# Turning keys and queries in 32 by 32 blocks on VectorE, with the stores to DRAM putting the blocks in place

## The chip, the cores and the metric

The kernel runs on one core of one Trainium2 chip. The metric is the device time of one execution in microseconds. The kernel before took 2872.75 us, the median of three runs from 2871.84 to 2873.47 us.

A core has TensorE (PE, matrix products; PEld is its weight load), VectorE (DVE), ScalarE (ACT), GpSimd (POOL) and SyncE (SP), which issues nearly all DMAs of this kernel. Sixteen DMA engines move the data. Products land in PSUM, from which ScalarE and VectorE empty them; the working memory is SBUF, 128 partitions wide.

## The reference

One layer of a hybrid encoder, for 2048 prompt tokens and for 8 sample sequences of 16 tokens, which share the weights:

```python
h = rms_norm(x, norm_g[l])
(a_x, a_b, a_c, a_z, g_q, g_f, g_i, g_z,
 s_q, s_k, s_v, s_z, m_a, m_b, m_c) = split_cols(h @ w_in[l])
...
q = rms_norm(s_q.reshape(B, T, SB_HEADS, SB_DH), q_norm_g[l])
k = rms_norm(s_k.reshape(B, T, SB_HEADS, SB_DH), k_norm_g[l])
v = s_v.reshape(B, T, SB_HEADS, SB_DH)
...
z = jnp.einsum('bqhd,bkhd->bhqk', qf, kf) * (1.0 / math.sqrt(SB_DH))
```

There are three branches: a gated convolution (A), a gated linear recurrence (B) and stick-breaking attention with 8 heads of 64 channels (C). Their outputs are projected, merged with sigmoid gates and projected once more. The normed keys and the values are outputs as well. This case is about `q` and `k`: they come out of their projection with tokens on the partitions, and the product `z` needs them with the channels there, so they have to be transposed.

## The kernel before, in words

The 17 tiles of 128 tokens (tile 0 holds the 128 sample tokens) are worked in three groups of 5, 6 and 6 tiles. For each group `run_jobs` goes through a list of projection jobs; each job has a slice of `w_in`, and runs over the group's two chunks of two or three tiles. A channel job (`proj_chan`, line 710) gives 128 channels by all tokens of a chunk; a token job (`proj_tok`, line 721) gives, for each tile, 128 tokens by 256 columns. Every product is made of three passes over high and low parts of the operands. Weights are loaded one job ahead (`wload`, lines 201 to 211): in group 0 from `w_in`, split there and stored (line 227), in later groups read back from that store.

Keys, values and queries are token jobs, two for each of them (`s` is the half of the columns, four heads), and in the list they alternate with channel jobs. `post_qk` is what follows a token job for keys or queries, once for each tile and half, 68 times in all. It squares and copies the accumulator on ScalarE, normalizes on VectorE (lines 819 and 820), and for keys stores the rows to the output. Then it turns the block: two transposes on TensorE with the unit matrix `idf` (line 826) into a PSUM tile, and `split` (lines 175 and 176) makes from that a high part on ScalarE and the rest on VectorE, both in the tile `kt`, which has two buffers. Two DMAs, one for each part, store it to the DRAM tensors `KT` or `QT` (line 830), with 512 contiguous bytes for each channel.

`post_qk` is a generator: it waits in the list `late` between its three steps, counted in the estimated cost of the products that go on meanwhile (`LATE`, 5 and 6 us), so that its instructions stand on their engines behind those of the tiles that follow. All instructions of an engine run in the order in which they are written, and so do SP's issues.

`KT` and `QT` are read in two places: by `load_step` (lines 281 to 287), which brings pieces of 64 channels by up to 512 tokens to the attention of the prompt, and by `whole` in `sample_attention` (line 404), which reads tile 0. The attention of the prompt runs as background work (`bg`) between the products of group 2 and of the merge.

Of the kernel before, what the change touches and what calls it, by code (L numbers as in the profile page):

```python
# [8 lines left out]
F32 = mybir.dt.float32  # L9
F32R = mybir.dt.float32r  # L10
# [6 lines left out]
P = 128  # L17
# [9 lines left out]
NTOK = NT * P  # L27
# [71 lines left out]
def trunk(ctx: ExitStack, tc: tile.TileContext, x_prompt, x_sample, cache_conv, state_hgrn, cache_k, cache_v,  # L99
# [3 lines left out]
    nc = tc.nc  # L103
# [25 lines left out]
    dram = ctx.enter_context(tc.tile_pool(name="dram", bufs=1, space=DRAM))  # L129
# [11 lines left out]
    def ps_tp(dt=F32):  # L141
        return pst[0].tile([P, 512], dt, tag="tp", name="tp")
# [4 lines left out]
    def ps_hg(dt=F32):  # L147
        return pst[0].tile([P, 512], dt, tag="hg", name="hg", bufs=1)

    KT = dram.tile([4, 2, P, NTOK], F32R, name="KT")
    QT = dram.tile([4, 2, P, NTOK], F32R, name="QT")
    VV = dram.tile([NTOK, 8, 64], F32, name="VV")

    OX = dram.tile([3, 4, 2, P, NTOK], F32R, name="OX")
# [5 lines left out]
    idf = const.tile([P, P], F32, name="idf")  # L162
# [10 lines left out]
    def split(hi, lo, src, eng=None):  # L173

        first = nc.scalar.copy(hi, src)  # L175
        return first, (eng or nc.vector).tensor_tensor(lo, src, hi.bitcast(F32), ALU.subtract)  # L176
# [91 lines left out]
    def load_step(m):  # L268

        if m >= len(steps) or m in held:  # L270
            return
        qi, pair, si, _, b0, b1, e = steps[m]
        qb = QBLOCKS[qi]
        h, nb = 2 * pair + e, b1 - b0
        q0, n = qb[0] * P, len(qb) * P
        if si == 0:
            Q1 = at.tile([P, 512], F32R, tag=f"Q1{e}", name="Q1", bufs=1)
            Q2 = at.tile([P, 512], F32R, tag=f"Q2{e}", name="Q2", bufs=1)
            for v in range(2):
                part = QT[pair, v, 64 * e:64 * e + 64, q0:q0 + n].bitcast(F32)  # L280
                nc.sync.dma_start(Q1[64 * v:64 * v + 64, :n].bitcast(F32), part)
                nc.sync.dma_start(Q2[64 - 64 * v:128 - 64 * v, :n].bitcast(F32), part)
        else:
            Q1, Q2 = held[m - 2][0:2]
        Kt = at.tile([P, 512], F32R, tag="Kt", name="Kt")
        for v in range(2):
            nc.sync.dma_start(Kt[64 * v:64 * v + 64, :nb * P].bitcast(F32),
                              KT[pair, v, 64 * e:64 * e + 64, (1 + b0) * P:(1 + b1) * P].bitcast(F32))
        if e == 0:
            Vt = at.tile([P, 4, 2, 64], F32, tag="Vt", name="Vt")  # L290
            nc.sync.dma_start(Vt[:, :nb], VV[(1 + b0) * P:(1 + b1) * P, h:h + 2].rearrange(
                "(b p) e c -> p b e c", p=P))
        else:
            Vt = held[m - 1][3]
        held[m] = (Q1, Q2, Kt, Vt)
# [93 lines left out]
    def sample_attention():  # L389
# [7 lines left out]
        S0 = slice(0, P)  # L397

        def whole(src, name):

            part = []
            for v in range(2):
                x = sa.tile([P, 4, P], F32, tag="cst", name=name, bufs=3)
                nc.sync.dma_start(x, src[:, v, :, S0].rearrange("h p t -> p h t").bitcast(F32))
                part.append(x)
            return part

# [2 lines left out]
        nc.gpsimd.memset(qz, 0.0)  # L410
        q0, q1 = whole(QT, "qw")
        for e in range(2):
# [136 lines left out]
        tp = ps_tp()  # L549
# [16 lines left out]
    qk = p1.enter_context(tc.tile_pool(name="qk", bufs=2))  # L566
# [242 lines left out]
    def post_qk(acc, t, s, gain, dst, rows_out, first_group):  # L809
        a3 = acc[:, :256].rearrange("p (h d) -> p h d", h=4)  # L810
        sq = qk.tile([P, 256], F32, tag="sq", name="sq", bufs=1)
        nc.scalar.activation(sq, acc[:, :256], AF.Square)
        kn = qk.tile([P, 4, 64], F32, tag="kn", name="kn", bufs=5)
        nc.scalar.copy(kn, a3)
        ssq = small.tile([P, 4], F32, tag="ssq4", name="ssq4")
        nc.vector.tensor_reduce(ssq, sq.rearrange("p (h d) -> p h d", h=4), AX.X, ALU.add)
        r = rstd_of(ssq, 4, 64)
        yield LATE[0]
        nc.vector.tensor_tensor(kn, kn, r.unsqueeze(2).broadcast_to([P, 4, 64]), ALU.mult)
        nc.vector.tensor_tensor(kn, kn, gain.unsqueeze(1).broadcast_to([P, 4, 64]), ALU.mult)  # L820
        if rows_out is not None:
            nc.sync.dma_start(rows_out[:, s * 256:(s + 1) * 256], kn.rearrange("p h d -> p (h d)"))
        yield LATE[1]
        tp = ps_tp() if first_group else ps_hg()
        for j in range(2):
            nc.tensor.transpose(tp[:, j * P:(j + 1) * P], kn[:, 2 * j:2 * j + 2].rearrange("p h d -> p (h d)"), idf)  # L826
        kt = qk.tile([P, 2, 2, P], F32R, tag="kt", name="kt", bufs=2)
        split(kt[:, 0], kt[:, 1], tp[:, :256].rearrange("p (j t) -> p j t", j=2))
        for v in range(2):
            nc.sync.dma_start(dst[2 * s:2 * s + 2, v, :, t * P:(t + 1) * P].rearrange("j p t -> p j t").bitcast(F32),  # L830
                              kt[:, v].bitcast(F32))

    def post_v(acc, t, s):
        vf = qk.tile([P, 256], F32, tag="kn", name="vf", bufs=5)
# [697 lines left out]
```

## Time and profile before

| | |
|---|---|
| median of 3 runs | 2872.75 us |
| time of the profiled execution | 2876.11 us |
| its span in the trace | 2873.2 us |
| TensorE busy | 2853.0 us, 99% |
| TensorE weight loads | 2662.3 us, 93% |
| VectorE busy | 1546.5 us, 54% |
| ScalarE busy | 1018.7 us, 35% |
| GpSimd busy | 331.8 us, 12% |
| DMA, hardware queue | 369,458 packets, 644.36 MB, 68.2% of 16 engines |
| transposes of line 826 | 136 products |
| stores to `KT` and `QT` | 136 DMAs of 128 KB |

In the lines of the trace, `out<-in` names the tensors by the program's names, `x` with a number is a count, and "L826" is the line of the kernel. A group of instructions shows its busy time in us, the mean of one in ns, and then the idle time of its engine just before them with what ended it. A window shows the busy time of each engine in a stretch of the span, the granted clock of TensorE, the mean busy share of the 16 DMA engines and the rate.

### The profile page before, as it was taken

The page shows a single profiled execution, that of the slowest core. Times are in us where ns is not written, and L with a number is a line of the kernel's source. Part 1 is how long each engine was busy: PE and PEld are TensorE (multiplying, and loading weights), DVE is VectorE, ACT ScalarE, POOL GpSimd, SP SyncE. Part 2 cuts the span into 40 slices and gives each one's busy share as a digit, 9 for nine tenths or more (in the row PEclk, how much of TensorE's full clock was granted, in tenths as well). Part 3 has the DMA queues.
Part 4 walks back from the last instruction along what each step waited for, and adds up shares of the span by engine and source line. Part 5 has one row for each costly group of instructions (what it writes and reads, how often), then busy time and mean ns, then how long its engine had stood idle before and what let it go on. Part 6 is the DMA issues. An engine that isn't in the chain of part 4 may idle for free.

```text
span 2873.2 us, 51723 instructions
## 1 busy us (share of the span) xinstructions
PE 2853.0 (99%) x19479; PEld 2662.3 (93%) x19479; DVE 1546.5 (54%) x3304; ACT 1018.7 (35%) x2375; POOL 331.8 (12%) x802
## 2 busy tenths in 40 slices
PE   9999999999999999999999999999999999999999
PEld 9999999999999999999999999999998888787888
DVE  5454635641344442545434747557485876867743
ACT  4333222242233332213334444434444444544420
POOL 3110000111200000001323111111010011010100
PEclk9999999999999999999999999999999999999999
DMA  8887777777678887746766454544447877878876
GB/s 306 305 276 247 231 241 244 231 243 243 212 249 266 276 265 243 243 167 192 237 215 202 146 173 136 173 139 151 144 145 238 286 234 239 266 250 266 271 250 210
DMA packets 370475, 649.76 MB, mean 226 GB/s; under 512 B 33481, under 2 KB 246306, under 8 KB 339506
## 3 DMA queue, kind: packets, MB, share of 16 engines
q1 hardware_dynamic: 369458, 644.36, 68.2%
q8 instruction: 154, 2.52, 0.4%
q0 software_dynamic: 768, 2.10, 0.2%
q14 instruction: 95, 0.78, 0.1%
HBM read 447.06 MB, written 199.27 MB: 225 GB/s over the span
## 4 chain that ended last, share of the span: by engine, by line
PE 76%; DVE 2%; DMA 2%; issue 1%; ACT 0%; POOL 0%; SPq 0%; DVEq 0%; POOLq 0%; ACTq 0%
PE acc L710 33%; PE acc L721 10%; PE acc L1440 9%; PE acc L1471 6%; PE pv L359 4%; PE tp L310 4%; PE z L330 2%; PE z L329 2%; PE z L1039 1%; PE tp L458 1%; DMA gate<-GM 1%; PE pv L522 1%; PE z L476 0%; PE hg L1086 0%; PE hg L826 0%
## 5 line engine op out<-in xcount | busy, mean ns | idle before, releaser
L710 PE MATMUL acc<-hx,w 128*128 128x384 f32 (+1 forms) x6816 | 1251.8, 333 | 0.1
L710 PEld LDWEIGHTS acc<-hx,w 128*128 128x128 f32 x6816 | 1106.5, 188 | 21.9 <-issue 15.2
L721 PE MATMUL acc<-w,hx 128*128 128x256 f32 x2544 | 328.6, 284 | 1.8 <-DVE hx L176 0.9
L342 DVE TENSOR_TENSOR_SCAN pr<-snb,carry 128x513 f32<-128x513 f32 x192 | 246.5, 1284 | 153.3 <-ACT snb L333 151.7
L721 PEld LDWEIGHTS acc<-w,hx 128*128 128x128 f32 x2544 | 310.9, 188 | 5.0 <-DVE hx L176 1.7
L311 ACT COPY aT<-tp 128x512 f32<-128x512 f32 (+2 forms) x320 | 167.6, 524 | 375.2 <-PE tp L310 361.3
L710 PE MATMUL acc<-hx,wst 128*128 128x384 f32 x1248 | 247.2, 344 | 0.0
L1440 PE MATMUL acc<-o,w 128*128 128x512 f32 (+2 forms) x1080 | 234.7, 363 | 1.8 <-DMA o<-OX 1.8
L333 ACT ACTIVATE snb<-z 128x512 f32<-128x512 f32 (+2 forms) x320 | 172.4, 539 | 144.5 <-PE z L330 140.4
L710 PEld LDWEIGHTS acc<-hx,wst 128*128 128x128 f32 x1248 | 215.4, 188 | 6.4 <-issue 3.7
L1440 PEld LDWEIGHTS acc<-o,w 128*128 128x128 f32 x1080 | 185.1, 188 | 33.8 <-issue 5.3
L347 DVE TENSOR_TENSOR sp<-sp,pr 128x512 f32<-128x512 f32 (+2 forms) x320 | 195.3, 611 | 29.2 <-POOL sp L338 3.7
L342 DVE TENSOR_TENSOR_SCAN pr<-snb,one 128x129 f32<-128x129 f32 (+3 forms) x128 | 114.4, 894 | 123.9 <-POOL snb L338 123.6
L310 PE MATMUL tp<-idf,sp 128*128 128x128 f32 x1088 | 171.3, 273 | 2.5 <-ACT aT L311 1.5
L335 ACT ACTIVATE sp<-z 128x512 f32<-128x512 f32 (+2 forms) x320 | 171.5, 536 | 0.0
L1471 PE MATMUL acc<-w,mh 128*128 128x256 f32 x816 | 161.2, 285 | 1.0 <-DVE yt L1479 0.8
L1176 ACT ACTIVATE gm<-acc 128x384 f32<-128x384 f32 (+1 forms) x144 | 68.2, 474 | 230.4 <-PE acc L710 197.5
L310 PEld LDWEIGHTS tp<-idf,sp 128*128 128x128 f32 x1088 | 131.8, 141 | 19.3 <-issue 4.4
L176 DVE TENSOR_TENSOR w<-wst,w 128x1024 fp32r<-128x1024 f32 x72 | 88.1, 1223 | 110.7 <-ACT w L175 107.9
L1471 PEld LDWEIGHTS acc<-w,mh 128*128 128x128 f32 x816 | 131.0, 188 | 7.2 <-issue 4.2
L329 PE MATMUL z<-Kt,Q 128*128 128x512 f32 (+2 forms) x320 | 128.8, 403 | 0.3 <-ACT sp L335 0.2
L359 PE MATMUL pv<-aT,Vt 128*64 128x512 f32 (+3 forms) x640 | 128.1, 535 | 0.0
(299 smaller groups left out, 3570.1 us busy)
## 6 DMA issues: line engine op xcount, KB each, us to landing
w<-W SPq DMA_DIRECT2D x168, 1024.0 KB, 6.0
W<-w SPq DMA_DIRECT2D x72, 1024.0 KB, 5.0
wst<-W SPq DMA_DIRECT2D x112, 512.0 KB, 5.1
wst<-in_w_in_dram SPq DMA_DIRECT2D x72, 512.0 KB, 5.1
GM<-gm SPq DMA_DIRECT2D x120, 192.0 KB, 3.7
W<-mwp SPq DMA_DIRECT2D x40, 512.0 KB, 4.2
Kt<-KT SPq DMA_DIRECT2D x160, 128.0 KB, 3.1
o<-OX SPq DMA_DIRECT2D x72, 256.0 KB, 4.7
```

What stands on the lines that cost most here:

```text
L310: nc.tensor.transpose(tp[:, j * P:(j + 1) * P], sp[:, j * P:(j + 1) * P], idf)
L311: nc.scalar.copy(aT[:, e, 0:nb, i * P:(i + 1) * P], tp[:, :w].rearrange("p (b q) -> p b q", q=P))
L329: nc.tensor.matmul(z[:, :w], Q1[:, i * P:(i + 1) * P], Kt[:, :w], start=True, stop=False)
L333: nc.scalar.activation(sn[:, 512 - w:512], z[:, :w], AF.Sigmoid, scale=-0.125)
L335: nc.scalar.activation(sp[:, :w], z[:, :w], AF.Sigmoid, scale=0.125)
L342: nc.vector.tensor_tensor_scan(pr[:, 512 - w:513][:, ::-1], s_in, s_in, one if diag else carry[e][i], ALU.mult, ALU.bypass)
L347: nc.vector.tensor_tensor(sp[:, :w], sp[:, :w], pr[:, 513 - w:513], ALU.mult)
L359: nc.tensor.matmul(pv[64 * e:64 * e + 64, c0:n], Vt[:, j, e], aT[:, e, j, c0:n], start=first and j == 0, stop=last and j == nb - 1, skip_g ...
L710: nc.tensor.matmul(acc[:, :n], w[0][a][:, k], hT[b][:, k, :n], start=k == 0 and i == 0, stop=k == KB - 1 and i == 2)
L721: nc.tensor.matmul(acc[:, :256], hT[b][:, k, ti * P:(ti + 1) * P], w[k // 4][a][:, k % 4], start=k == 0 and i == 0, stop=k == KB - 1 and i ...
L1440: nc.tensor.matmul(acc[:, :n], w[0][a][:, k, dd * P:(dd + 1) * P], box[x][b][:, k, sl], start=k == 0 and i == 0, stop=k == 3 and i == 2)
L1471: nc.tensor.matmul(acc[:, :256], box["l" if b else "h"][:, k, ti * P:(ti + 1) * P], w[k // 4][a][:, k % 4], start=k == 0 and i == 0, stop= ...
```

## The change

`post_qk` makes no products any more. VectorE transposes the 128 by 256 block in 32 by 32 blocks from one SBUF tile to another: what lands at partition 32a + q and column 32x + t is the element of token 32a + t and channel 32x + q. `split` then works from SBUF. The blocks are still in the wrong place, and the stores put them right: one DMA for each of the four values of `a` takes 32 partitions and writes, for each channel and each part, 32 tokens, 128 contiguous bytes. So a block leaves in four DMAs instead of two. The dimensions of `KT` and `QT` are put in another order, so that part, column pair and quarter become one step in DRAM; a channel's row of tokens is as long as before. The readers follow the new order, and `whole` reads in two halves.

```diff
-    KT = dram.tile([4, 2, P, NTOK], F32R, name="KT")
-    QT = dram.tile([4, 2, P, NTOK], F32R, name="QT")
+    KT = dram.tile([2, 2, 2, P, NTOK], F32R, name="KT")
+    QT = dram.tile([2, 2, 2, P, NTOK], F32R, name="QT")
...
-                part = QT[pair, v, 64 * e:64 * e + 64, q0:q0 + n].bitcast(F32)
+                part = QT[pair // 2, v, pair % 2, 64 * e:64 * e + 64, q0:q0 + n].bitcast(F32)
...
-                              KT[pair, v, 64 * e:64 * e + 64, (1 + b0) * P:(1 + b1) * P].bitcast(F32))
+                              KT[pair // 2, v, pair % 2, 64 * e:64 * e + 64, (1 + b0) * P:(1 + b1) * P].bitcast(F32))
...
-                nc.sync.dma_start(x, src[:, v, :, S0].rearrange("h p t -> p h t").bitcast(F32))
+                for s in range(2):
+                    nc.sync.dma_start(x[:, 2 * s:2 * s + 2], src[s, v, :, :, S0].rearrange("j p t -> p j t").bitcast(F32))
...
         yield LATE[1]
-        tp = ps_tp() if first_group else ps_hg()
-        for j in range(2):
-            nc.tensor.transpose(tp[:, j * P:(j + 1) * P], kn[:, 2 * j:2 * j + 2].rearrange("p h d -> p (h d)"), idf)
-        kt = qk.tile([P, 2, 2, P], F32R, tag="kt", name="kt", bufs=2)
-        split(kt[:, 0], kt[:, 1], tp[:, :256].rearrange("p (j t) -> p j t", j=2))
-        for v in range(2):
-            nc.sync.dma_start(dst[2 * s:2 * s + 2, v, :, t * P:(t + 1) * P].rearrange("j p t -> p j t").bitcast(F32),
-                              kt[:, v].bitcast(F32))
+
+        kx = qk.tile([P, 2, 256], F32, tag="kt", name="kx", bufs=2)
+        nc.vector.transpose(kx[:, 1], kn.rearrange("p h d -> p (h d)"))
+        split(kx[:, 0].bitcast(F32R), kx[:, 1].bitcast(F32R), kx[:, 1])
+        for a in range(4):
+            place = dst[s, :, :, :, t * P + 32 * a:t * P + 32 * a + 32].bitcast(F32)
+            nc.sync.dma_start(place.rearrange("v j (c q) t -> q (v j c) t", q=32),
+                              kx[32 * a:32 * a + 32].rearrange("q v (x t) -> q (v x) t", t=32))
```

## The prediction

> **What bounds the kernel now.** I read the page's head and busy shares first, then the chain that ended last by engine, then the same chain in order of time in a stretch where keys are projected.
>
> ```profile
> span 2873.2 us, 51723 instructions
> PE 2853.0 (99%) x19479; PEld 2662.3 (93%) x19479; DVE 1546.5 (54%) x3304; ACT 1018.7 (35%) x2375; POOL 331.8 (12%) x802
> ...
> PE 76%; DVE 2%; DMA 2%; issue 1%; ACT 0%; POOL 0%; SPq 0%; DVEq 0%; POOLq 0%; ACTq 0%
> ...
> 660.36 0.22 PE hg L826 x2
> 660.58 1.43 PE acc L721 x12
> 662.01 1.06 PE acc L710 x6
> 663.07 0.22 PE hg L826 x2
> ```
>
> TensorE is busy for all but 20.2 us of the span, and the chain goes through it. The two transposes of one block of keys or queries (line 826) stand on that chain with 0.22 us, back to back with projection products: nothing covers them. So what leaves TensorE shortens the span, unless something else then makes it wait. The candidate is the DMA side, so I read six windows, from the first to the last store of keys or queries in each group of tokens (group 0 keys, queries; group 1; group 2):
>
> ```profile
> core 0: us, PE busy (x) PEld busy (x) DVE busy (x) ACT busy (x) POOL busy (x), PEclk, DMA share, GB/s
> 62.00:104.00 42.00, 41.63 (x331) 41.26 (x330) 19.27 (x38) 16.05 (x37) 7.20 (x12) 1.00 0.92 310
> 130.00:172.00 42.00, 41.72 (x333) 41.31 (x332) 20.76 (x38) 15.84 (x34) 10.14 (x14) 1.00 0.86 289
> 630.00:686.00 56.00, 56.00 (x450) 54.83 (x449) 18.92 (x44) 17.21 (x45) 9.61 (x16) 1.00 0.81 255
> 745.00:800.00 55.00, 55.00 (x488) 53.60 (x488) 16.96 (x41) 16.78 (x46) 11.64 (x18) 1.00 0.70 218
> 1375.00:1434.00 59.00, 59.00 (x445) 56.88 (x444) 30.47 (x63) 23.19 (x63) 17.85 (x34) 1.00 0.79 244
> 1498.00:1554.00 56.00, 56.00 (x442) 54.37 (x442) 25.14 (x53) 21.36 (x59) 18.75 (x35) 1.00 0.72 222
> ```
>
> TensorE is full in all six, and VectorE and ScalarE are half idle. The DMA engines (next to last column) are the second fullest resource, and fullest just where the change puts its new stores. The capacity left free, window by share left, is 3.4, 5.9, 10.6, 16.5, 12.4 and 15.7 us. The first two windows hold 10 blocks each (5 tiles by 2 column halves), the other four 12: 68 in all.
>
> **The change part by part.** *Removed from TensorE:* 136 transposes with their weight loads, in 68 pairs of 0.22 us: 15.0 us off the chain. That is the whole possible gain, 0.52%.
>
> *Vector and scalar work.* The rows nearest to what is added and moved, by form:
>
> ```profile
> L342 DVE TENSOR_TENSOR_SCAN pr<-snb,one 128x257 f32<-128x257 f32 x32 | 24.7, 772 | 18.2 <-POOL snb L338 17.9
> L819 DVE TENSOR_TENSOR kn<-kn,rr 128x256 f32<-128x256 f32 x68 | 29.1, 428 | 91.9 <-POOL rr L234 90.5 <-ACT aT L311 1.4
> L176 DVE TENSOR_TENSOR kt<-hg,kt 128x256 fp32r<-128x256 f32 x48 | 20.1, 419 | 37.6 <-ACT kt L175 37.3
> L176 DVE TENSOR_TENSOR ob<-ob,oh 128x256 fp32r<-128x256 f32 x32 | 13.6, 426 | 12.2 <-ACT oh L175 12.2
> L175 ACT CAST kt<-hg 128x256 fp32r<-128x256 f32 x48 | 17.9, 372 | 36.4 <-PE hg L826 36.1 <-DMA QT<-kt 0.3
> L175 ACT CAST oh<-ob 128x256 fp32r<-128x256 f32 x32 | 13.0, 405 | 32.2 <-DVE ob L1117 32.1
> ```
>
> The trace shows no VectorE transpose. On 128x256 an elementwise operation takes 0.43 us and a scan 0.77 us; I take 0.43, since a transpose, too, reads and writes each element once, and keep 0.77 as the upper bound. That is 29 to 53 us more VectorE work over 68 blocks. The split into two parts now reads SBUF, as `ob` does: 0.03 us more on ScalarE, 0.01 on VectorE. VectorE is at 131.5 of 310 us in the six windows, so I cost these at nothing on the path; what hides them is the projection of the next tile (two pieces of 1.43 us, 2.86 us). Were that cover gone, 68 times 0.46 us, 31 us, would show.
>
> The Trainium skill (VectorE: DVE Perf Modes, "The three transpose paths") says that VectorE turns 32 by 32 blocks only, and gives 311 ns for 128x128 bf16. No run so far shows it. Two such, 0.62 us as an estimate, would lie between my bounds, and the sum would stay.
>
> *SP's queue.* Four issues for each block instead of two, and four more DMAs in `whole` (the same bytes in halves): 140 more. In group 0 one of these issues holds SP for 0.36 to 1.2 us.
>
> ```profile
> L830 SPq DMA_DIRECT2D KT<-kt x20: 359/475/1203, 63.2 to 99.1; - x20
> ...
> KT<-kt SPq DMA_DIRECT2D x68, 128.0 KB, 4.2
> QT<-kt SPq DMA_DIRECT2D x68, 128.0 KB, 3.7
> w<-W SPq DMA_DIRECT2D x168, 1024.0 KB, 6.0
> ```
>
> Behind them on SP stand the next weights (lines 201, 208 and 211). Two issues at 0.475 are 0.95 us for each block of 2.86 us of projection. I count this as part of the DMA price below and not twice, because an issue of 1.2 us where others take 0.36 is SP being held while transfers run.
>
> *The stores themselves* decide. Before, a block leaves in 512 packets of 512 bytes (two parts, two column pairs, 128 rows). After, it leaves in 2048 packets of 128 bytes, because a row of a turned block is 32 tokens long. Bytes are equal, and 104,448 packets come on top. No transfer of 128-byte rows is in the trace, so I price a packet from the hardware queue's row in three windows (the line above them is that of the whole span):
>
> ```profile
> DMA packets 370475, 649.76 MB, mean 226 GB/s; under 512 B 33481, under 2 KB 246306, under 8 KB 339506
> ...
> ## 3 DMA queue, kind: packets, MB, share of 16 engines
> q1 hardware_dynamic: 11808, 12.95, 91.2%
> ...
> q1 hardware_dynamic: 10158, 12.58, 91.1%
> ...
> q1 hardware_dynamic: 4941, 11.58, 88.2%
> ```
>
> The first is 62 to 104 us, the other two 40 us each, from 80 and from 2200. In the last two, half the packets with nearly the same bytes take nearly the same share: 46.3 and 48.7 us of engine time per MB. So down to 512 bytes a packet costs its bytes. The first window gives 47.3 us per MB, which is 24.2 ns for 512 bytes. For 128 bytes the lower end is bytes alone, 6.1 ns, and nothing is added; a cost below that is excluded, since the bytes stay. The upper end is the mean packet of the first window, 0.912 x 42 x 16 / 11,808, 51.9 ns. I take 24.2 ns: the nearest row is the 512-byte packet, and I assume that a shorter one costs as much.
>
> Then a block takes 2048 x 24.2 ns / 16 = 3.10 us of all engines, against 0.78 us before: 2.32 us more. The windows get 23.2, 23.2 and four times 27.9 us; less the free capacity, 19.8, 17.3, 17.3, 11.4, 15.5 and 12.2 us overflow, 93.5 us in sum. Weights queue behind this. How late they may be: they are asked for one job ahead and land in 6.0 us; a channel job lasts two chunks of four pieces of 1.06 us, 8.5 us, and a token job six tiles of 2.86 us, 17.2 us, so the lead is 2.5 or 11.2 us. I take the middle, 6.8 us, once for each window, 41 us. What is left, about 53 us, TensorE waits.
>
> Sum: 53 - 15 = +38 us. The span of 2873.2 us becomes 2911; the span is within 0.5 us of the median of the runs, 2872.75, while the profiled execution as a whole took 2876.11. So I forecast 2911 us. With leads of 2.5 and 11.2 us it would be +64 and +11.
>
> What a page says of short packets stands by itself. The Trainium skill (DMA: Bandwidth & Descriptors, "Specifications") puts the minimum for line rate at 512 B and says that below it the engine does a read-modify-write: this speaks against the change, and no run so far shows it. The same page ("Why small descriptors are slow") counts a beat per 32 bytes and three cycles per packet; at its 850 MHz 128 bytes take 8.2 ns, an estimate that no row here reaches down to, by which nothing would overflow and the time would be 2858 us.
>
> **The rivals.** *1. Packets cost their bytes.* With 6.1 ns, or anything under 18 ns, the added transfer fits into the free capacity and the leads but for 9 us at most, and the transposes' 15 us come off: 2858 us, up to 2867. For it: the two windows with 46.3 and 48.7 us per MB. Against it: they stop at 512 bytes, and the first two windows have 3.4 and 5.9 us free. It is the opposite sign, and it decides at 18 ns: there a block costs 1.53 us more, and 5.1 and 2.6 us are left over in group 0 and 1 us in group 1; at 20.3 ns it is 21 us in all.
>
> *2. The two staging buffers.* The gain is there, but the third block of a chunk waits until the first block's store has landed.
>
> ```profile
> ACT kt L175 <- DMA QT<-kt: 5.7, 3, 2.2
> ...
> ACT kt L175 <- DMA KT<-kt: 0.7, 2, 0.4
> ```
>
> These waits (60 to 200 us; the total, the count and the longest) say that two buffers just suffice now: 0.37 + 0.42 + two issues of 0.37 + 4.2 us landing are 5.7 us, and two tiles are 5.7 us. After, it is 0.43 + 0.41 + 0.43 + 1.5 for four issues + 4.2 + 2.3, 9.3 us, so the third transpose holds VectorE for 3.6 us; behind it on VectorE stand the split, which ScalarE waits for, and the gates, and behind those the emptying of the accumulator. Two accumulators cover one tile, 2.86 us; 0.7 us by the 20 chunks of three tiles is 14 us and eats the gain: 2872 us. With no cover it would be 72 us, 2930.
>
> *3. The mean price.* At 51.9 ns a block costs 5.87 us more, the overflow after leads is about 294 us, and the time 3152 us. For it only that a shorter packet might wait as long as a long one in a full queue; against it the flat price per MB.
>
> **How the numbers follow.** Forecast, 20.3 to 33 ns (at 33 it is +115 us): 0.40, its own range 2879 to 2988. Rival 1: 0.37. Rival 2, and prices of 18 to 20.3 ns: 0.13. Above 33 ns, up to rival 3: 0.10. So slower 0.50, faster 0.37, the same 0.13; 0.2%, 5.7 us, is about what a measurement of this kernel can tell from no change. Cases of both signs hold most of the chance, so the range reaches from rival 1's end, 2857, to 2990, and leaves out rival 3.
>
> **What would show it.** Line 826 and its 136 products are gone from TensorE; were they still there, nothing holds. VectorE has 68 transposes of 0.43 to 0.77 us. The packets under 512 bytes rise from 33,481 by 139,264. The step on the price: the hardware queue's share by packets in the same six stretches. If those stretches keep their length less 2 us each and the DMA share stays below 0.95, the price is near bytes, and I am wrong by rival 1. If they grow by 5 to 15 us with TensorE idle until weights (`w`, `wst`) arrive, the forecast holds. If VectorE's waits for the stores grow instead and the share has room, it is rival 2.

## The result and the profile after

The changed kernel takes 2998.48 us (median of 4 runs, 2998.39 to 2999.72) against 2873.11 us for the kernel before on the same chip: a ratio of 1.0435, 95% interval 1.0417 to 1.0453, 125 us slower. The profiled execution's span is 2996.8 us; the one before was 2873.2. All ratios here are of undisturbed executions: three of e11's twelve (3,589 us and twice 9,917) and one of the kernel before beside e16 (10,802 us) lie far outside and are not counted.

From the page of the changed kernel: the span, the busy times, the granted clock by slices, the packets and the hardware queue (packets, MB, share of 16 engines).

```profile
span 2996.8 us, 51676 instructions
...
PE 2891.7 (96%) x19343; PEld 2676.6 (89%) x19343; DVE 1572.4 (52%) x3372; ACT 1015.5 (34%) x2375; POOL 327.0 (11%) x802
...
PEclk9889999999999999999989999999999999999999
...
DMA packets 477164, 649.78 MB, mean 217 GB/s; under 512 B 174985, under 2 KB 352994, under 8 KB 446194
...
q1 hardware_dynamic: 476146, 644.37, 67.1%
```

The 136 products are gone (19,343 for 19,479), and yet TensorE is busy 38.7 us longer. It is idle for 105.1 us where it was idle for 20.2, that is 84.9 us more; 84.9 and 38.7 are the 123.6 us between the spans. The longer busy time is a lower clock: the mean granted clock is 0.983 where it was 1.000, and 2891.7 x 0.983 = 2842.5 us is within 5 us of the 2838.0 that were left to do (2853.0 less the 15.0 of the transposes). The digits fall to 8 in the first stores' stretches and once more later, where all were 9 before. The hardware queue has 106,688 packets more, and a smaller share. 104,448 of them are the shorter rows; the other 2,240 are 16 for each of the 140 DMAs that came on top (e6, with as many more DMAs and long rows, has just these 2,240, and e12, with 4 more, has 64). Packets under 512 bytes rose by 141,504: the 139,264 that were said, and these.

What ended TensorE's longest waits, from the view of all waits (us in sum, times, longest); first the largest group before, then the four largest now:

```profile
PE tp L629 <- DVE xt L619: 2.6, 4, 1.2
```

```profile
PE acc L722 <- ACT w L175: 14.3, 4, 5.8
PE acc L711 <- ACT w L175: 14.3, 3, 10.7
PE acc L711 <- DMA w<-W: 13.0, 1, 13.0
PE tp L310 <- DVE sp L347: 12.0, 11, 2.2
```

Weights end most of it: 28.6 us in 7 waits for ScalarE's split of the first group's weights, and 21.7 us in 6 waits for loads of `w` and `wst`. In the longest of the 7, 10.7 us from 205.0 on, ScalarE itself waits for a `wst` that SP asked for behind 20 stores. Another 12.0 us are waits of the attention for VectorE.

The six stretches from the first store of keys or queries to the last (about 272 us in sum before, by the issues; 463 us now, rounded outward to 495 here): length, busy time of each engine, clock, DMA share, GB/s.

```profile
57.00:123.00 66.00, 55.03 (x388) 53.26 (x387) 26.19 (x56) 17.38 (x40) 9.60 (x16) 0.92 0.67 175
146.00:213.00 67.00, 52.17 (x384) 50.98 (x382) 25.58 (x52) 17.01 (x39) 12.97 (x19) 0.92 0.63 167
662.00:744.00 82.00, 75.46 (x616) 71.80 (x615) 30.05 (x69) 21.48 (x58) 13.20 (x22) 1.00 0.62 157
790.00:874.00 84.00, 71.91 (x584) 67.37 (x582) 27.11 (x65) 19.81 (x55) 15.66 (x25) 0.96 0.55 139
1444.00:1544.00 100.00, 90.89 (x597) 79.24 (x596) 46.10 (x93) 33.54 (x91) 23.43 (x51) 0.91 0.58 154
1587.00:1683.00 96.00, 82.10 (x555) 73.74 (x554) 41.03 (x87) 29.97 (x84) 27.98 (x56) 0.93 0.55 140
```

From store to store each stretch has grown by more than a half, and the DMA share is 0.55 to 0.67 where it was 0.70 to 0.92. Not all of the growth is lost time: the stores now end later, and the six stretches hold 3,124 products where the prediction's six held 2,489. Lost are the 67.4 us for which TensorE stands still in them, of 105.1 in the whole run. So most of the time was lost in the stretches that the prediction named, but not because the DMA engines were full.

One such place in full. First SP's issues (start, length, what, how many), then TensorE with the idle time before it and what ended it, then the clock (next to the last two columns) around it, all of the changed kernel.

```profile
838.03 0.45 SPq L208 DMA_DIRECT2D w<-W  x1
842.40 10.88 SPq L831 DMA_DIRECT2D QT<-kx  x8
...
859.98 7.60 SPq L831 DMA_DIRECT2D QT<-kx  x8
...
868.23 2.07 SPq L831 DMA_DIRECT2D QT<-kx  x4
...
870.95 0.38 SPq L208 DMA_DIRECT2D w<-W  x1
```

```profile
863.14 0.86 PE L523 MATMUL pv<-vc,at__9334 128*32 128x128 f32 x24
876.96 6.13 PE L711 MATMUL acc<-hx,w 128*128 128x384 f32 x23 [12.96 <-DMA w<-W]
```

```profile
860.00:864.00 4.00, 4.00 (x43) 1.00 0.56 98
864.00:877.00 13.00, 0.04 (x2) 0.63 0.66 164
877.00:880.00 3.00, 3.00 (x10) 0.50 0.52 171
880.00:885.00 5.00, 5.00 (x30) 0.89 0.92 317
```

Between two loads of weights SP holds the 20 stores of five blocks, for 33 us. Each store waits for its block, and these blocks come late, one at a time, behind other work of VectorE and ScalarE. The weights are asked for at 870.95; TensorE has stood since 864.00 and goes on at 876.96. Then it runs at a granted clock of 0.50 for 3 us and 0.89 for 5.

The same two loads in the kernel before, and then one of the late blocks in the changed kernel, which VectorE had turned at 842.29:

```profile
776.92 0.33 SPq L208 DMA_DIRECT2D w<-W  x1
777.55 4.88 SPq L830 DMA_DIRECT2D QT<-kt  x4
782.51 0.42 SPq L208 DMA_DIRECT2D w<-W  x1
```

```profile
848.95 0.37 ACT L1208 COPY vg<-acc 128x256 f32<-128x256 f32 x1 [2.07 <-PE acc L722]
849.22 0.41 ACT L175 CAST kx<-kx 128x256 fp32r<-128x256 f32 x1
...
849.66 0.43 DVE L176 TENSOR_TENSOR kx<-kx 128x256 fp32r<-128x256 f32 x1 [6.94 <-ACT kx L175]
```

Before, two blocks stood there, and the loads were 5.6 us apart. ScalarE's half of the late block stands behind the copy of an accumulator that TensorE had first to fill, and VectorE waits 6.94 us for that half. The number of blocks is not all of it: five between two loads is the most in the kernel before too, at other places, but there they take 16 to 19 us (three times) and here 31 to 33 (three times).

Nothing in this place is full (while TensorE stands, the DMA share is 0.66). It is a question of what stands behind what, so a word on where the order comes from: it is not that of the program text, but is written by the framework's planner, which lays out each engine's instructions before the kernel reaches the chip. That it goes by priorities and by its own reckoning of how long each operation takes is a reading that fits the runs below, in which a store's pattern alone changes the order; its reckoning itself is not on record. With the change it wrote another order, also for instructions that the change does not touch. Leaving the blocks' own instructions out, of the order before these many instructions are out of sequence (the longest common sequences taken away):

```
kernel                                        VectorE  ScalarE      SP
                                             of 3,102 of 2,124 of 1,868
changed kernel                                    41      116     166
e1: VectorE, two stores of 512 B rows              5       10      31
e2: TensorE, the four stores of the change        44      104     153
e3: TensorE, four stores, 32 partitions, 512 B    28       66     139
e6: TensorE, four stores, 128 partitions, 512 B   16       25      83
e9: changed kernel planned as long rows           14       38      75
e11: the same, later groups only                   5        6      53
e12: new arrangement in DRAM only                  5        6       8
```

The counts on ScalarE and SP depend on how like instructions are told apart (another way gives 80 and 145 for the changed kernel); the ranking does not. TensorE's products move as well: 324 of 17,949 in the changed kernel, 338 in e2 and 210 in e3, but 20 to 30 in e1, e6, e9, e11 and e12.

What the order does to the blocks can be read from the traces. From the end of ScalarE's copy of an accumulator (`kn`) to the end of VectorE's half of the block it takes, in the mean of 68 blocks, 15.9 us before, 4.8 in e1, 7.1 in e9, 17.3 in e3, 21.0 in the changed kernel and 26.8 in e2. In the changed kernel the longest is 41.8 us.

### The profile page after: what moved, and what is told of

Read it like the earlier page. It is cut to its first block, busy times and chain, and to the rows that moved or that the text cites. A ratio compares the mean times of both kernels' runs of the same rounds, so it can differ in the third digit from the quotient of the medians.

```text
span 2996.8 us, 51676 instructions
## 1 busy us (share of the span) xinstructions
PE 2891.7 (96%) x19343; PEld 2676.6 (89%) x19343; DVE 1572.4 (52%) x3372; ACT 1015.5 (34%) x2375; POOL 327.0 (11%) x802
## 3 DMA queue, kind: packets, MB, share of 16 engines
q1 hardware_dynamic: 476146, 644.37, 67.1%
## 4 chain that ended last, share of the span: by engine, by line
PE 85%; DVE 4%; DMA 3%; issue 3%; ACT 2%; POOL 2%; SPq 1%; DVEq 0%; POOLq 0%; ACTq 0%
PE acc L711 41%; PE acc L722 10%; PE acc L1441 9%; PE acc L1472 7%; PE pv L359 4%; PE tp L310 4%; PE z L330 2%; PE z L329 2%; PE z L1040 2%; POOL rr L234 1%; PE tp L459 1%; DVE pr L342 1%; DMA wst<-in_w_in_dram 1%; SPq L831 1%; PE pv L523 1%
## 5 line engine op out<-in xcount | busy, mean ns | idle before, releaser
L722 PEld LDWEIGHTS acc<-w,hx 128*128 128x128 f32 x2544 | 317.8, 193 | 32.9 <-ACT w L175 15.2
L310 PEld LDWEIGHTS tp<-idf,sp 128*128 128x128 f32 x1088 | 133.3, 143 | 34.6 <-issue 13.2
L359 PE MATMUL pv<-aT,Vt 128*64 128x512 f32 (+3 forms) x640 | 137.9, 551 | 2.7 <-ACT aT L311 2.7
```

What stands on the lines that cost most here:

```text
L310: nc.tensor.transpose(tp[:, j * P:(j + 1) * P], sp[:, j * P:(j + 1) * P], idf)
L359: nc.tensor.matmul(pv[64 * e:64 * e + 64, c0:n], Vt[:, j, e], aT[:, e, j, c0:n], start=first and j == 0, stop=last and j == nb - 1, skip_g ...
L722: nc.tensor.matmul(acc[:, :256], hT[b][:, k, ti * P:(ti + 1) * P], w[k // 4][a][:, k % 4], start=k == 0 and i == 0, stop=k == KB - 1 and i ...
```

## The experiments

Theory A: the 128-byte packets are slow. Theory B: the order that was written is slow. Rivals for the rest: the four issues on SP, VectorE as a link between `kn` and the stores, the two staging buffers, the arrangement in DRAM.

**e1: VectorE transposes, stores as before.** The block is turned on VectorE, and left unplaced by two stores with rows of 512 bytes.

```diff
-        for a in range(4):
-            place = dst[s, :, :, :, t * P + 32 * a:t * P + 32 * a + 32].bitcast(F32)
-            nc.sync.dma_start(place.rearrange("v j (c q) t -> q (v j c) t", q=32),
-                              kx[32 * a:32 * a + 32].rearrange("q v (x t) -> q (v x) t", t=32))
+        for v in range(2):
+            nc.sync.dma_start(dst[s, v, :, :, t * P:(t + 1) * P].rearrange("j p t -> p j t").bitcast(F32),
+                              kx[:, v].rearrange("p (j t) -> p j t", j=2))
```

> The VectorE transposes and the split stay as in the changed kernel, but a block leaves as before, in two DMAs of 256 packets of 512 bytes; the putting of the blocks in place is left out, so keys and queries are misplaced. Packet theory (the 128-byte packets cost the time): everything is back but the transposes' gain is kept, about 2860 us. Issue theory (four issues for a block hold SP): about 2860 us too. Order theory (in the written order of SP's queue the weight loads stand behind stores of blocks that are late; here 33 of 352 loads stand at least one block further back than before, in the changed kernel 32): well above 2873 us, 2920 to 3000.

Measured: 2896.67 us, 1.0080 (1.0063 to 1.0097). It is 22 us slower than before, although 15.0 us of TensorE are gone and the stores are as they were. The transpose itself, from the view of the staging tile (ns min/median/max), and the longest group of waits, from the view of all waits (us in sum, times, longest):

```profile
L827 DVE STREAM_TRANSPOSE kx<-kn x68: 435/445/447, 53.2 to 1557.9; 128x256 f32<-128x256 f32 x68
```

```profile
ACT kx L175 <- DVE kx L827: 189.0, 66, 5.6
```

The transpose takes 0.445 us, as costed. But ScalarE, which makes the high part, arrives at 66 of 68 blocks before VectorE has turned them, and stands there for 189 us in sum, with its other work behind it; before, it stood 38.6 us in 38 waits for TensorE's transposes. TensorE feels it at the accumulators that ScalarE has not yet copied, which it never waited for before:

```profile
PE acc L722 <- ACT kn L815: 8.5, 15, 0.9
...
PE acc L711 <- ACT kn L815: 4.3, 6, 1.4
```

That is 12.8 of the 25.0 us that TensorE is idle more than before. All three theories missed, the order theory too. It had counted weight loads that stand further back behind stores, and there are 33 of them here, one more than in the changed kernel, at a loss of only 22 us. In e9 below there are 33 as well. So the place of the loads alone does not cost the time; what differs is how late the blocks are that stand before them (4.8 and 7.1 us against 21.0).

**e2 and e3: transposes back on TensorE, four stores.** e2 keeps the stores of the change; e3 lets each of the four take 32 whole rows, 128 packets of 512 bytes.

```diff
+        tp = ps_tp() if first_group else ps_hg()
+        for j in range(2):
+            nc.tensor.transpose(tp[:, j * P:(j + 1) * P], kn[:, 2 * j:2 * j + 2].rearrange("p h d -> p (h d)"), idf)
-        nc.vector.transpose(kx[:, 1], kn.rearrange("p h d -> p (h d)"))
-        split(kx[:, 0].bitcast(F32R), kx[:, 1].bitcast(F32R), kx[:, 1])
+        split(kx[:, 0].bitcast(F32R), kx[:, 1].bitcast(F32R), tp[:, :256])
...
# e3 only
-            nc.sync.dma_start(place.rearrange("v j (c q) t -> q (v j c) t", q=32),
-                              kx[32 * a:32 * a + 32].rearrange("q v (x t) -> q (v x) t", t=32))
+            nc.sync.dma_start(dst[s, :, :, 32 * a:32 * a + 32, t * P:(t + 1) * P].bitcast(F32).rearrange("v j q t -> q (v j) t"),
+                              kx[32 * a:32 * a + 32].rearrange("q v (j t) -> q (v j) t", t=P))
```

> TensorE transposes as before, but the stores of the changed kernel, four DMAs of 512 packets of 128 bytes (from rows that are already in place, so that keys and queries are misplaced). Packet theory and issue theory: as slow as the changed kernel plus the 15 us of the transposes, about 3013 us. Order theory (24 loads further back instead of 32): 2950 to 3000. If the VectorE transposes were the cause: 2873.

> TensorE transposes as before, four DMAs for a block with 128 packets of 512 bytes each, all in place: the number of issues without the short packets. Packet theory: 2873 us. Issue theory: about 3000 us. Order theory (23 loads further back): 2940 to 3000, close to the run with the short packets.

Measured: e2 3010.52 us (1.0478), as the packet and issue theories had it and above the order theory's range; e3 2909.49 us (1.0122), which none had. At first sight the 101 us between them are the price of short packets. They are not: the written order is another one too (the table above), and the next runs hold it fixed.

**e4: the stores written later.** One more `yield 6.0` ahead of the four stores of the changed kernel, so that fewer weight loads stand behind them on SP: 11 loads are a block or more further back than before, where the changed kernel has 32.

> The changed kernel with its four stores traced 6 us of product cost later, so that they stand behind the next weight loads (11 of 352 loads further back than before instead of 32). Same packets, same issues. Packet and issue theory: 2998 us, unchanged. Order theory: most of the loss gone, 2870 to 2920 us; below 2873 only if what is left of the packets' cost is under the 15 us of the transposes.

Measured: 2979.92 us (1.0369), 18.6 us below the changed kernel and far above the order theory's 2870 to 2920. Fewer loads stand back, but the blocks are later still (23.6 us in the mean against 21.0). This order was written anew as well: against the changed kernel's, 216 products, 42 instructions on VectorE and 39 on ScalarE are out of sequence. So the 18.6 us are not the price of the loads' place alone.

**e5: the changed kernel's order, long packets.** The program is planned as the change has it; afterwards the address patterns of the 272 stores are exchanged, and nothing else.

```diff
...
+            row, a = o.ap[0][0], o.offset // 32 % 4
+            oap = (o.ap[0], (128 * row, 4), (1, 128))
+            kap = (k.ap[0], (128, 4), (1, 128))
+            ooff = o.offset - 32 * a + 32 * a * row
+            block.instructions[i] = replace(x, outs=[replace(o, ap=oap, offset=ooff)], ins=[replace(k, ap=kap, offset=k.offset)])
```

> The changed kernel instruction for instruction, in its own written order, waits and queues; only the address patterns of the 272 stores are put in afterwards, so that a store writes 32 whole rows in 128 packets of 512 B instead of 512 packets of 128 B (the same bytes; putting the blocks in place is left out). Theory A, the packets: a store of 512 short packets is itself slow, whatever the order: about 2895 to 2925 us, that is most of the 101 us between the two TensorE kernels comes back. Theory B, the written order: the planner reckons short-packet stores as long and writes another order of loads, blocks and evictions, and that order costs the time even where the stores are quick: 2980 to 3000 us, as the changed kernel.

Measured: 2995.57 us, 1.0425 (1.0408 to 1.0442). Taking all short packets out of the changed kernel gives back about 3 us, less than the two intervals can tell apart. The page of this run:

```profile
span 2993.6 us, 51676 instructions
...
PE 2891.0 (97%) x19343; PEld 2675.0 (89%) x19343; DVE 1573.0 (53%) x3372; ACT 1016.3 (34%) x2375; POOL 326.7 (11%) x802
...
q1 hardware_dynamic: 371698, 644.37, 65.5%
```

TensorE's row is that of the changed kernel within a microsecond. Theory A falls.

**e6 and e7: a good order, both kinds of packets.** TensorE transposes, four stores per block of one part and one head pair from all 128 partitions. e7 is e6 with the address patterns exchanged after planning, 512 packets of 128 bytes to a store.

```diff
# e6, against e3
-            nc.sync.dma_start(dst[s, :, :, 32 * a:32 * a + 32, t * P:(t + 1) * P].bitcast(F32).rearrange("v j q t -> q (v j) t"),
-                              kx[32 * a:32 * a + 32].rearrange("q v (j t) -> q (v j) t", t=P))
+            nc.sync.dma_start(dst[s, a // 2, a % 2, :, t * P:(t + 1) * P].bitcast(F32),
+                              kx[:, a // 2, (a % 2) * P:(a % 2 + 1) * P])
# e7, after planning
+            oap = (o.ap[0], (32, 4), (1, 32))
+            kap = (k.ap[0], (64, 4), (1, 32))
...
```

> Transposes on TensorE, four stores per block, one for each part and head pair, from all 128 partitions, 128 packets of 512 B each; values as in the reference. Baseline for the next run. Both theories: as the kernel with four stores from 32 partitions, 2909 us, within 10 us.

> The run before it, instruction for instruction in the same written order; only the address patterns of the stores are put in afterwards, so that each store moves the same 64 KB in 512 packets of 128 B (values misplaced). Theory A, the packets: 80 to 110 us above the run before it, near 3000 us. Theory B, the written order: within 10 us of the run before it, near 2912 us.

Measured: e6 2881.46 us, 1.0024 (1.0013 to 1.0035), e7 2893.89 us, 1.0075 (1.0059 to 1.0092). e6 was expected at 2909 by both theories and came out 28 us lower: with stores of 512-byte rows from 128 partitions the order is nearer to that of before than with such stores from 32, though the stores themselves differ too. Two more issues per block, with the transposes still on TensorE and in an order slightly different from that of before, thus cost 7 us. The short packets cost 12 us in an order that is the same to the instruction: a little more than the 10 of theory B, far from the 80 to 110 of theory A. For e6 and then for e7, the page, and from the staging tile's view SP's issues of the key stores (min/median/max in ns):

```profile
span 2883.6 us, 51950 instructions
...
q1 hardware_dynamic: 371698, 644.37, 67.7%
```

```profile
L832 SPq DMA_DIRECT2D KT<-kx x136: 319/422/1198, 63.2 to 1443.0; - x136
```

```profile
span 2889.6 us, 51950 instructions
...
q1 hardware_dynamic: 476146, 644.37, 69.7%
```

```profile
L832 SPq DMA_DIRECT2D KT<-kx x136: 359/504/3016, 63.3 to 1456.7; - x136
```

Shares times spans times 16 engines are 31,235 and 32,225 us of engine time: 990 us for 104,448 more packets, 9.5 ns for each; between e5 and the changed kernel, in the same way, 801 us and 7.7 ns. With 24.2 ns for a 512-byte packet, one of 128 bytes comes to (24.2 + 3 x 9.5) / 4 = 13.2 ns, or 11.8 by the other pair.

**e8: the stores on ScalarE's queue.** `nc.scalar.dma_start` in place of `nc.sync.dma_start` in the changed kernel.

> The changed kernel with its 272 short-packet stores issued from ScalarE's queue instead of SP's, nothing left out; the order is planned anew. Theory Q, the stores hold up the weight loads behind them on SP's queue: 2870 to 2910 us. Theory A, the packets on the transfer engines: 2960 us or more. ScalarE pays 272 issues of 0.5 us, 136 us of its idle time, so some 20 us may come from ScalarE waiting at a store.

Measured: 2937.68 us (1.0224), between the two ranges. Away from SP the stores no longer hold up the weights, but ScalarE issues them late, and now the staging buffers hold up the blocks: VectorE stands 70.2 us in 28 waits for stores to land before it can turn the next block, and ScalarE 33.2 us in 8 before it can write its half. The order was planned anew as well, so this run bounds nothing exactly.

**e9 and e10: the changed kernel in an order planned for long rows.** Planned with four stores of every fourth row, 128 partitions and 512 bytes, which all read the block when it is complete; after planning, each gets the pattern of the change. Nothing is left out. In e10 VectorE also writes the high part.

```diff
# while planning
+            place = dst[s, :, :, :, t * P:(t + 1) * P].bitcast(F32)
+            nc.sync.dma_start(place.rearrange("v j (r a) t -> a (v j r) t", a=4)[a], kx[:, 1, (a % 2) * P:(a % 2 + 1) * P])
# after planning
+            oap = ((row, 32), (32 * row, 16), (1, 32))
+            kap = (k.ap[0][:1] + (32,), (32, 16), (1, 32))
...
# e10
-        split(kx[:, 0].bitcast(F32R), kx[:, 1].bitcast(F32R), kx[:, 1])
+        nc.vector.tensor_copy(kx[:, 0].bitcast(F32R), kx[:, 1])
+        nc.vector.tensor_tensor(kx[:, 1].bitcast(F32R), kx[:, 1], kx[:, 0], ALU.subtract)
```

> The changed kernel's own instructions and its own 272 stores of 512 packets of 128 B, nothing left out, but the order is written by the planner as if each store took 128 packets of 512 B from all 128 partitions (the address patterns of the change are put in afterwards). Theory B, the written order costs the time: the kernel with two long-row stores took 2897 us; two more issues per block cost 7 us (2881 against 2874) and the short packets 3 to 12 us, so 2900 to 2920 us. If the packets or the four issues cost the time whatever the order: 2980 us or more.

> The run before it, with the rounded half of each block also written by VectorE (one operation of some 0.43 us more on VectorE for each of 68 blocks, one fewer on ScalarE). Theory C: what is left of the loss is ScalarE standing at its half of a block until VectorE's transpose is done (189 us in 66 waits in the kernel with two long-row stores), with its part of the weights' split behind it: 15 us or more below the run before it. Rival: ScalarE has room for these waits, and VectorE's 29 us more are hidden as well: within 6 us of the run before it.

Measured: e9 2907.95 us, 1.0116 (1.0099 to 1.0133): 90 us below the changed kernel, with the same work, the same stores and the same 476,146 packets on the hardware queue. Theory B holds: the order that was written is slow. The page of e9:

```profile
span 2907.2 us, 51703 instructions
...
PE 2850.7 (98%) x19343; PEld 2653.8 (91%) x19343; DVE 1575.9 (54%) x3372; ACT 1015.1 (35%) x2375; POOL 326.7 (11%) x802
...
q1 hardware_dynamic: 476146, 644.37, 69.2%
```

SP's issues in e9 at the same loads (the last two are those between which the changed kernel held 20 stores):

```profile
791.36 0.38 SPq L208 DMA_DIRECT2D w<-W  x1
...
794.30 3.42 SPq L831 DMA_DIRECT2D QT<-kx  x4
...
799.58 9.54 SPq L831 DMA_DIRECT2D QT<-kx  x12
809.22 0.43 SPq L208 DMA_DIRECT2D w<-W  x1
810.62 5.93 SPq L831 DMA_DIRECT2D QT<-kx  x8
...
817.20 0.38 SPq L208 DMA_DIRECT2D w<-W  x1
```

Between the last two stand 8 stores, and they are 8 us apart, where it was 20 stores and 33 us. The two before them have 16 stores and 18 us between them, and TensorE's longest wait in the whole run is 4.57 us instead of 12.96. e10 is 2897.60 us, 1.0082 (1.0065 to 1.0099), 10 us below e9: neither the 15 us of theory C nor the 6 us of its rival, and the intervals touch. TensorE's waits for accumulators that ScalarE has not copied (`kn`) fall from 20.2 us in 21 waits to 6.3 in 5, as the theory has it.

**e11 to e16: what remains.** e11 leaves the first group's 20 blocks on TensorE with two stores, as before, and treats the other 48 as e10 does. e12 is the kernel before with the new arrangement of `KT` and `QT` and their readers alone. e13 and e14 are e11 and e10 with three staging buffers, and e16 is the kernel before with that exchange. (e15, a first form of e16 that gave the sample attention's own `kt` a third buffer too, needs more SBUF than there is and has no time.)

```diff
# e11
+        if first_group:
+            tp = ps_tp()
...
+            split(kx[:, 0].bitcast(F32R), kx[:, 1].bitcast(F32R), tp[:, :256])
+            for v in range(2):
+                nc.sync.dma_start(dst[s, v, :, :, t * P:(t + 1) * P].rearrange("j p t -> p j t").bitcast(F32),
+                                  kx[:, v].rearrange("p (j t) -> p j t", j=2))
+            return
# e13, e14 (vf and vr, which share the tag, likewise); e16 has the same for kt
-        kx = qk.tile([P, 2, 256], F32, tag="kt", name="kx", bufs=2)
+        kx = qk.tile([P, 2, 256], F32, tag="kt", name="kx", bufs=3)
-        kn = qk.tile([P, 4, 64], F32, tag="kn", name="kn", bufs=5)
+        kn = qk.tile([P, 4, 64], F32, tag="kn", name="kn", bufs=4)
```

> The changed kernel with 20 of the 68 blocks (the first group's keys and queries) still turned on TensorE and put down by two stores with 512-B packets, as before; the other 48 turned on VectorE, both halves written by VectorE, put in place by four stores of 128-B packets, planned as long rows like the two runs before. Nothing left out. Its order differs from that of before in 30 of 17,855 matmuls and 6 of 2,124 ScalarE instructions. If the written order is what the change paid for: 48 x 0.22 us of TensorE, 10.6 us, come off, and two more issues for 48 blocks cost some 5 us: 2864 to 2876 us, so at or below the kernel before. If the change's parts have a price of their own (four stores, VectorE as a link of the chain): 2885 us or more.

> The kernel before with only the new arrangement of the two DRAM arrays (head pairs innermost but one) and the reads that follow it: transposes on TensorE, two stores of 128 packets x 2 of 512 B per block, the same written order on every engine. All theories: within 6 us of the kernel before. If it is 15 us or more slower, the arrangement in DRAM has a share in every kernel of this study.

> The run with the later groups' 48 blocks on VectorE, with three staging buffers for the turned block instead of two (paid for by one buffer fewer for the normalised rows). In that run VectorE stood 11.0 us in 9 waits for key stores and 6.7 us in 5 for query stores to land before it could write the next block. Staging theory (the second rival of the prediction): these waits go and 4 to 10 us with them, 2868 to 2874 us. Rival, they are covered: 2876 to 2880 us.

> The run with all 68 blocks turned and halved on VectorE and the order planned as for long rows, with three staging buffers instead of two and one buffer fewer for the normalised rows. VectorE waited 16.2 us there for key stores to land. Staging theory: 8 to 20 us below it, 2878 to 2890 us. Rival: within 6 us of its 2897.6 us.

> The kernel before with the same exchange of buffers as in the two runs with a third staging buffer (three for the turned block, four for the normalised rows). A control: within 3 us of the kernel before by every theory, since it waits only a few microseconds in all for its stores to land; if it is 4 us or more faster, the third buffer gains without the VectorE version too.

Measured, as ratios to the kernel before: e11 1.0006 (0.9997 to 1.0016), e12 1.0001 (0.9992 to 1.0010), e13 0.9998 (0.9989 to 1.0007), e14 1.0058 (1.0043 to 1.0074), e16 1.0001 (0.9992 to 1.0011). e11 lies at the upper end of what was expected if the order is what was paid for, e13 in the range of the staging theory and e14 at the edge of its rival's. The arrangement in DRAM costs nothing. With the first group back on TensorE the loss is gone, but nothing is gained: the 10.6 us that come off TensorE are paid back elsewhere. In the profiled execution TensorE is idle for 28.2 us, 8.0 more than before, and busy for 2849.4, 7.0 more than the 2842.4 that were left to do. The waits for the staging buffers are real, as VectorE's timeline of e11 shows:

```profile
658.22 0.42 DVE L821 TENSOR_TENSOR kn<-kn,kg_bc 128x256 f32<-128x256 f32 x1
661.32 0.45 DVE L836 STREAM_TRANSPOSE kx<-kn 128x256 f32<-128x256 f32 x1 [2.68 <-DMA KT<-kx]
...
662.47 0.41 DVE L817 TENSOR_REDUCE ssq<-sq 128x4 f32<-128x256 f32 x1
```

Behind the waiting transpose stands `ssq` of the next tile, for that ScalarE waits with its next square and the copy of an accumulator behind it, and TensorE stands for 2.34 us (from 661.33 on). A third buffer cuts VectorE's waits for stores from 12.5 us in 10 waits to 3.5 in 4 (e11 to e13) and from 23.5 in 14 to 2.5 in 4 (e10 to e14). (The 17.7 us that the expectation for e13 puts on VectorE hold 5.2 us of ScalarE's; the 16.2 for e14 leave out the stores to `QT`.) The times come down by about 2 and 6 us, but each pair of intervals overlaps, so the gain is likely and not shown. No version was found that beats the kernel before; e11 and e13 tie with it.

## Why the prediction was wrong

The sign was right by luck; the time, 2911 us against 2998 us, was not, and the working named the wrong cause. With the measured price of a packet (below) the prediction's own sum leaves no overflow and gives 2858 us, the other sign. One path leads from the kernel before to the changed one: 2874 (before), 2897 (e1: VectorE transposes), 2908 (e9: four stores of 128-byte packets), 2998 (the order planned for them). The last step changes the order alone. The first two are close to one thing each, but e1 and e9 have orders of their own, near that of before.

*The products.* 15.0 us off TensorE: right as far as it can be seen. e2 is 12.0 us above the changed kernel, in an order that is not quite the same.

*VectorE's transposes, "cost nothing on the path".* The duration was right, 0.436 us for the 0.43 taken and below the estimate of 0.62. The cover was not. It was reckoned as room on VectorE, of which there was plenty. What costs, as far as the runs show, is the chain VectorE, ScalarE, VectorE on two in-order engines: ScalarE's 189 us of waits in e1, and behind them TensorE's for accumulators. e1 is 22 us slower with 15 us less TensorE work, so this step, put at zero (31 us without any cover), costs about 37 us. In e10, without ScalarE in the chain, it is likely some 10 us less; e11, which leaves it out of the first group, where ScalarE and VectorE have the weights to split as well, is 22 us less again (ratio 1.0082 to 1.0006; some 3 of these, 20/68 of the 11 us between e1 and e9, are that group's stores). Not tested is whether the chain would be covered if the blocks were written as far behind their accumulators as before (15.9 us) and not at once (4.8).

*SP's queue, counted within the DMA price.* The issue of a short-packet store takes 0.50 us, near the 0.475 taken. The two more issues are a cost of their own, about 7 us (e6, with a little of another order in it), a small one.

*The price of a packet.* Taken 24.2 ns, measured 11.8 to 13.2. The added engine time is 990 / 68 / 16 = 0.91 us per block (0.74 by the other pair) and not 2.32: a window gets 9.1 or 10.9 us more. The first two have 3.4 and 5.9 us free and the third 10.6; what is over, 5.7 us at most, is within the lead of 6.8. In e7 the fullest stretch, the first, has a DMA share of 0.92. The price is below the 18 ns at which rival 1 was to decide, and in e7 short packets in a given order do cost only 12 us. So rival 1's premise held and its time, 2858, did not, because it too left the rest of the kernel in place. The Trainium skill (DMA: Bandwidth & Descriptors, "Why small descriptors are slow") led to 8.2 ns: nearer than my row, and 4 to 5 ns too low. Its rule in "Specifications", that below 512 bytes a read-modify-write follows, shows here in no more than those 8 to 10 ns for each added packet.

*The overflow less the lead, 53 us of waiting.* That TensorE waits for weights is what the trace shows for 50.3 us of its waits; its cause is not a full DMA but loads that stand on SP behind stores of blocks that come late. This is the failed step, and the unsaid one under it: that every other instruction keeps its place. 90 us of the 125 come from the order that was written (e9 against the changed kernel), which no term stood for. Loads stand behind stores as often in e9 (33) as in the changed kernel (32); what the slow order adds is that the blocks are late too, 21.0 us behind their accumulators against 7.1. (Before they were 15.9 behind, but with no load standing back for them.) This reading fits the runs; none of them makes the blocks late and leaves the rest of the order alone. The prediction's own test put growing stretches and a share with room to spare in two different cases; both came together.

*Rival 2, the staging buffers.* In the changed kernel VectorE waits for stores only 6.8 us in 4 waits. This becomes visible when other waits go (e8, e11), in e13 and e14 worth a few microseconds at most.

*Rival 3* (51.9 ns a packet, 3152 us) fell with the price.

What stays open: which property of a store makes the planner write the slow order, beyond what the orders show (nearest to before with 128 partitions and long rows, further with 32, furthest with 32 and short rows); and how the 90 us divide among the engines' orders. e4 and e8, each in another order again, give no clean share.

## What to carry over

When a planner writes the order, a changed operation is paid for twice: for what it takes on the chip, and for what it does to the place of everything else. Compare the written orders before pricing anything, and hold the order fixed (exchange the patterns after planning) before calling an operation slow. Where stretches grow and no engine and no queue is full, look for late requests: follow one idle interval of the bounding engine back through the in-order streams, and ask whether a request stands behind many things or behind late ones. An engine with half its time free can still cost time as one more link in a chain, because those that wait for it stop what stands behind them.

## What the runs showed of the hardware

The first surprise is how cheap short packets are: four times as many, of 128 bytes, add 8 to 10 ns of engine time each and 0.08 us to an issue (422 to 504 ns), in all 0.4% of this kernel. The second is what a stall costs beyond itself: after the 13 us of idle time shown above TensorE came back at a granted clock of 0.50 for 3 us and 0.89 for the next 5. The Trainium skill (TensorE: Matmul & The Clock Gate, "Part 1: The HAM clock gate") says that an idle window of some 3.4 us halves the clock and that as long a busy one restores it; 0.50 agrees, and 0.89 over 5 us is 1.1 us more at half rate, 4.1 us in all. Over the changed kernel, 84.9 us more idle time came with 53.7 us (38.7 + 15.0) of slower products. In e9, whose stalls are under 5 us each, 36.3 us more idle time came with 12.7 us (2850.7 less 2838.0): a smaller share, as one would expect if short stalls leave the clock alone, which these two kernels alone don't prove.
